# Decoder trunk on one core: carried state times C as 128-row products, decay and norm sums on VectorE, the last scaling moved

## The chip, the cores and the metric

One core of a Trainium2 chip runs the whole program. The metric is the device time of one execution in microseconds (us). The kernel before takes 1945.37 us (median of three runs, 1945.06 to 1946.57). Engines: TensorE (PE; its weight loads are PEld), VectorE (DVE), ScalarE (ACT), GpSimd (POOL), SyncE (SP, which here only issues DMAs).

## The reference

A decoder layer on a sequence of 1024 tokens with 1024 channels: layer norm, one large input projection, two token mixers side by side (a convolution branch and a Mamba-2 state space branch), a gated sum, an output projection, and a gated feed-forward block with a short convolution. The part that matters here is the state space branch, in chunks of 128 tokens, for 32 heads of 64 channels in 4 groups that share B and C:

```python
a_cs = jnp.cumsum(a, axis=-1)
decay = where(causal, exp(a_cs[..., :, None] - a_cs[..., None, :]), 0.0)
cb = einsum("bclgn,bcsgn->bcgls", cc, bc)
y_diag = einsum("bcgrls,bcsgrp->bclgrp", cb[:, :, :, None] * decay, xs)
states = einsum("bclgn,bcgrl,bclgrp->bcgrpn", bc, decay_states, xs)
...  # carry: prev = chunk_decay * prev + states
y_off = einsum("bclgn,bcgrpn,bcgrl->bclgrp", cc, prev, exp(a_cs))
return y_diag + y_off
```

`y_off` is the state carried in from the chunks before, times C, times a decay that depends on head and token. Behind it: the skip term, the gate silu(z), and an RMS norm over each group of 512 channels. In the convolution branch a layer norm over 1024 channels follows a convolution with 31 taps.

## The kernel before

The tokens are worked in two halves of 512. Activations lie transposed (channels on partitions, tokens along the free axis). Every large product is three products of float32r parts (`mm3`, L192 to L194): high times high, high times low, low times high. So a weight tile of 128x1024 is loaded by SP, its high part cast by ACT (L158) and its low part subtracted by DVE (L163; in the second half many low parts come back from DRAM). TensorE needs both.

`mixers(hh, hT)` runs the four groups of a half: projections of B, C, x with their short convolution (`conv4`), the gate z, the two halves of the convolution branch's GLU, and then `ssd_group` with four chunks. In a chunk (first half 0, second half 1; names such as m_3_1 are group and chunk):

- `px` (L646) transposes x, `pb` (L649, L650) transposes B and makes C times B.
- `ab` (L640) is a DMA that spreads the cumulated decays of 8 heads over all partitions. ACT makes the decay matrix `m` from it (L653 eight times Relu, L660 Exp), DVE multiplies it by the masked C times B (L685).
- For all but the very first chunk, ACT makes `ce` = exp(ab) (L663) and POOL multiplies it by C (L664), 128x1024.
- `py` (L690, L693): for each head, 64 output rows: the diagonal part from `xs` and `m`, then the carried part from the state `S` and `ce`, accumulated in the same PSUM bank. Two heads of a pair lie on the two halves of the output partitions.
- `pn` (L192 to L194) is the chunk's new state; DVE scales S by the chunk's decay (L702) and adds it (L705).
- DVE adds the skip term (L708, four times 128x128), multiplies by the gate (L719), ACT squares (L721), DVE sums (L722, L723).

`scaled()` of a group makes the norm: TensorE sums over partitions (L730), ACT takes the root, DVE the reciprocal (L739, `rows`), POOL issues two DMAs that send the row to DRAM and spread it over the partitions (L741, L742, `rstd`), and DVE scales x with it (L745, four times 128x512). `parts()` splits the result into high and low (ACT L759, DVE L760). In groups 1 to 3 `scaled` of the group before is called ahead of the group's chunks, and its L745 is bound behind the skip of chunk 0 by a list `held`. Group 3's own `scaled` and `parts` are called in the loop over the last gate columns, at j = 4. The next phase, `gated`, begins with the gate_b weights (`w_gb`).

The 31-tap convolution runs as 480 single operations on DVE (L577, 128x512, taps named c<-vl), which `fill` puts behind other work in small numbers (table `FILL`). `conv_norm` loads the eight convolved blocks of a half, sums them for the mean, and sums their squares (POOL: L869, L871, L881).

A scheduler sets each engine's order from the program's order, the priorities and its own estimates; the engines work their lists strictly in order. PSUM has two pools of four banks: `acc` for the projections, `sm` for everything small.

Of the kernel before, what the change touches and what calls it, by code (L numbers as in the profile page):

```python
# [8 lines left out]
F32 = mybir.dt.float32  # L9
F32R = mybir.dt.float32r  # L10
AF = mybir.ActivationFunctionType
# [52 lines left out]
def kernel(  # L64
# [557 lines left out]
    def ssd_group(pl, hh, g, xT, BT, CT, zs):  # L622
# [10 lines left out]
        for c in range(4):  # L633
# [25 lines left out]
                )  # L659
            exps.append(A.activation(out=m, in_=m, func=AF.Exp, scale=-1.0))  # L660
            if not first:
                ce = pl.tile([P, 8, P], F32, tag="ce", name=f"ce{nm}")
                A.activation(out=ce, in_=ab, func=AF.Exp)  # L663
                G.tensor_tensor(  # L664
                    out=ce, in0=ce, in1=CT[:, cs].unsqueeze(1).to_broadcast([P, 8, P]), op=ALU.mult
                )
            cbm = pl.tile([P, P], F32, tag="cbm", name=f"cbm{nm}")
            V.tensor_mul(cbm, pb[:, P : 2 * P], upper)
# [18 lines left out]
            for i in range(4):  # L687
                pair = [(2 * i + k, py[k * HP : (k + 1) * HP, i * P : (i + 1) * P]) for k in (0, 1)]
                for h, o in pair:
                    TE.matmul(o, xs[:, h * HP : (h + 1) * HP], m[:, h, :], start=True, stop=first)  # L690
                if not first:
                    for h, o in pair:
                        TE.matmul(  # L693
                            o, S[:, h * HP : (h + 1) * HP], ce[:, h, :], start=False, stop=True
                        )
            if not last:
                pn = bank(0)
                mm3(pn, lambda i: bt[:, i, :], lambda i: xsd[:, i, :], True, True)
# [7 lines left out]
            for i in range(4):  # L706
                k = PC_SD + 4 * g + i
                skip = V.scalar_tensor_tensor(  # L708
                    out=xT[:, i, cs],
                    in0=xT[:, i, cs],  # L710
                    scalar=pc[:, k : k + 1],
                    in1=py[:, i * P : (i + 1) * P],
                    op0=ALU.mult,
                    op1=ALU.add,
                )
            fill(FILL[hh][1], skip)
            while held and c == 0:
                issue_after(held.pop(), skip)
            V.tensor_mul(xT[:, :, cs], xT[:, :, cs], zs[:, :, cs])  # L719
            sq = pl.tile([P, 4, P], F32, tag="sq", name=f"sq{nm}")  # L720
# [62 lines left out]
    def mixers(hh, hT):  # L783
        pre = first_columns(hh, hT, (CT_B, CT_C, CT_X))
        with pool(f"mixers{hh}") as pl:
            time_steps(pl, hh, pre[0])
            scaled = parts = None
            for g in range(GROUPS):
                BT = conv4(pl, hh, column(hh, hT, CT_B + g) if g else pre[1], 16 + g)
                CT = conv4(pl, hh, column(hh, hT, CT_C + g) if g else pre[2], 20 + g)  # L790
                xT = pl.tile([P, 4, HALF], F32, tag="x4", bufs=2, name=f"x4_{hh}_{g}")
                for i in range(4):
                    j = 4 * g + i
                    conv4(pl, hh, column(hh, hT, CT_X + j) if j else pre[3], j, xT[:, i, :])
                zs = z_gate(pl, hh, hT, g)
                for i in (2 * g, 2 * g + 1):
                    glu(pl, hh, hT, i)
                    conv31(hh, i)
                if g:
                    scaled()  # L800
                if g == 1:
                    yT = big_tile(f"yT{hh}_0")
                if g in (1, 2):
                    parts(yT)
                split_2 = parts
                scaled, parts = ssd_group(pl, hh, g, xT, BT, CT, zs)
                if g == 3:
                    ssm_out_first(pl, hh, yT)
                    yT = big_tile(f"yT{hh}_2")
                    split_2(yT)  # L810
                    gate_first(pl, hh, hT, range(3))
            for j in range(3, 8):
                gate_first(pl, hh, hT, (j,))
                fill(FILL[hh][2], los[-1])
                if j == 4:
                    scaled()
                    parts(yT)
        return yT

    def gated(pl, hh, hT, yT, during):  # L820
# [37 lines left out]
    def conv_norm(pl, hh, place):  # L858

        squares = pl.tile([P, 2, HALF], F32, tag="sq", name=f"csq{hh}")  # L860
        stats = pl.tile([P, 2, HALF], F32, tag="stats", name=f"stats{hh}")
        mean, var = stats[:, 0, :], stats[:, 1, :]
        n = 8
        pairs = [pl.tile([P, 2, HALF], F32, tag=f"c{i}", name=f"cc{hh}_{i}") for i in range(n // 2)]
        cs = []
        for i in range(n):
            G.dma_start(pairs[i // 2][:, i % 2, :], c_scr[hh][i])
            cs.append(pairs[i // 2][:, i % 2, :])
        G.tensor_add(mean, cs[0], cs[1])  # L869
        for c in cs[2:]:  # L870
            G.tensor_add(mean, mean, c)  # L871
        pm = bank(0)
        TE.matmul(pm, mean_w, mean, start=True, stop=True)
        for i, c in enumerate(cs):
            V.tensor_tensor(out=c, in0=c, in1=pm, op=ALU.subtract)
            if i == 0:
                A.activation(out=var, in_=c, func=AF.Square)
            else:
                sq = squares[:, i % 2, :]
                A.activation(out=sq, in_=c, func=AF.Square)  # L880
                G.tensor_add(var, var, sq)  # L881
        return lambda: conv_silu(pl, cs, var, place)

    def conv_silu(pl, cs, var, place):
# [677 lines left out]
```

## Time and profile before

| | |
|---|---|
| median of three runs | 1945.37 us (1945.06 to 1946.57) |
| profiled execution | 1946.6 us, its span 1944.9 us |
| granted TensorE clock, mean | 0.997 |
| PE busy | 1920.8 us, 99% |
| DVE busy | 1640.9 us, 84% |
| ACT busy | 1104.3 us, 57% |
| POOL busy | 221.7 us, 11% |
| DMA | 398.44 MB, 205 GB/s over the span |

The span runs from the first to the last instruction of the profiled execution. A row of the view of groups reads: line, engine, operation, out<-in, shapes, count | busy us, mean ns of one | idle time of the engine just before them and what ended it. A row of the timeline reads: start, duration, engine, line, operation, and in brackets the idle time before it. The chunks of the first half lie between about 97 and 430 us, those of the second between 630 and 985, `gated` of the second half begins near 1024.

### The profile page before, as it was taken

The numbers are of one execution on the slowest core, as the hardware profiler recorded it, in microseconds if no ns is written. First come the engines' busy times: TensorE is split into PE (matmuls) and PEld (weight loads), VectorE is DVE, ScalarE is ACT, GpSimd is POOL, SyncE is SP. The second block draws the span as 40 slices with busy tenths as digits, with TensorE's granted clock in tenths as the row PEclk, the third lists the DMA queues.
The fourth block names the chain that finished last, engine by engine and source line by source line (L and its number), as shares of the span: only waits on it lengthen the run. The fifth ranks groups of instructions, "written<-read, shape, count | busy, mean of one in ns | idle before, by whom it ended". The sixth has DMA issues, their size and how long they took to land.

```text
span 1944.9 us, 26118 instructions
## 1 busy us (share of the span) xinstructions
PE 1920.8 (99%) x9452; PEld 1576.9 (81%) x9452; DVE 1640.9 (84%) x2278; ACT 1104.3 (57%) x1648; POOL 221.7 (11%) x275
## 2 busy tenths in 40 slices
PE   9999999999999999999999999999999999999998
PEld 8887888788878888878777888888888888888886
DVE  7488999897998698989978787787788888889778
ACT  6586777654525777776532535365555555553534
POOL 1001011011000111110112250011000000022010
PEclk9999999999999999999999999999999999999999
DMA  6655565547486565554464474776445555479673
GB/s 231 217 187 205 204 208 177 177 167 282 180 280 212 198 220 205 192 208 171 162 224 162 149 241 176 247 260 238 156 163 200 174 176 187 162 266 368 205 243 114
DMA packets 138194, 398.44 MB, mean 205 GB/s; under 512 B 16432, under 2 KB 16976, under 8 KB 138064
## 3 DMA queue, kind: packets, MB, share of 16 engines
q1 hardware_dynamic: 116928, 335.39, 50.0%
q0 software_dynamic: 14656, 49.83, 7.1%
q10 hardware_dynamic: 6480, 11.55, 1.6%
q8 instruction: 74, 1.21, 0.3%
q14 instruction: 56, 0.46, 0.1%
HBM read 300.61 MB, written 96.09 MB: 204 GB/s over the span
## 4 chain that ended last, share of the span: by engine, by line
PE 44%; issue 3%; DMA 2%; DVE 2%; ACT 0%; POOL 0%; DVEq 0%; ACTq 0%; POOLq 0%; SPq 0%
PE acc L194 8%; PE acc L192 8%; PE acc L193 8%; PE sm L192 7%; PE sm L193 7%; PE sm L194 7%; DMA st_wo<-wo 1%; DMA rstd<-nrm_scr 1%; DMA first_scr<-first 0%; DVE x L745 0%; DVE c L577 0%; DMA rb<-wup 0%; POOL ce L664 0%; DMA nrm_scr<-rows 0%; DVE yT_l L760 0%
## 5 line engine op out<-in xcount | busy, mean ns | idle before, releaser
L192 PE MATMUL acc<-hT_h,w_c 128*128 128x512 f32 x1000 | 391.4, 391 | 0.8 <-ACT w_c L158 0.8
L194 PE MATMUL acc<-hT_h,w_c 128*128 128x512 f32 x1000 | 389.9, 391 | 0.4 <-DMA w_c<-low_scr 0.4
L193 PE MATMUL acc<-hT_l,w_c 128*128 128x512 f32 x1000 | 390.0, 390 | 0.0
L577 DVE SCALAR_TENSOR_TENSOR c<-vl,pc,c 128x512 f32<-128x512 f32 x480 | 376.4, 805 | 6.8 <-ACT c L566 2.7
L192 PEld LDWEIGHTS acc<-hT_h,w_c 128*128 128x128 f32 x1000 | 187.8, 188 | 41.7 <-issue 1.4
L194 PEld LDWEIGHTS acc<-hT_h,w_c 128*128 128x128 f32 x1000 | 187.8, 188 | 39.8 <-DMA w_c<-low_scr 0.9
L193 PEld LDWEIGHTS acc<-hT_l,w_c 128*128 128x128 f32 x1000 | 187.8, 188 | 38.8 <-issue 0.3
L158 ACT CAST w_c<-st_c 128x1024 fp32r<-128x1024 f32 x128 | 133.8, 1046 | 131.0 <-PE acc L194 88.3
L664 POOL TENSOR_TENSOR ce<-ce,xbc 128x1024 f32<-128x1024 f32 x28 | 72.7, 2597 | 495.0 <-ACT ce L663 495.0
L1287 ACT CAST w_dn<-dr 128x1024 fp32r<-128x1024 f32 (+1 forms) x72 | 67.3, 943 | 75.7 <-DVE dr L1220 39.8
L192 PE MATMUL sm<-h1s,w_s 128*128 128x512 f32 x264 | 102.8, 389 | 0.5 <-ACT fuv L1130 0.5
L163 DVE TENSOR_TENSOR w_c<-st_c,w_c 128x1024 fp32r<-128x1024 f32 x62 | 76.9, 1240 | 30.6 <-ACT w_c L158 30.5
L193 PE MATMUL sm<-h1s,w_s 128*128 128x512 f32 x264 | 102.7, 389 | 0.0
L194 PE MATMUL sm<-h1s,w_s 128*128 128x512 f32 x264 | 102.2, 389 | 0.0
L653 ACT ACTIVATE m<-ab,acs 128x128 f32<-128x128 f32 x256 | 78.3, 391 | 26.5 <-PE sm L690 24.8
L1288 DVE TENSOR_TENSOR w_dn<-dr,w_dn 128x1024 fp32r<-128x1024 f32 (+1 forms) x72 | 77.7, 1087 | 4.7 <-ACT w_dn L1287 4.6
L527 DVE SCALAR_TENSOR_TENSOR x<-u,pc,x 128x512 f32<-128x512 f32 x96 | 74.8, 793 | 3.6 <-ACT x L525 3.5
L194 PE MATMUL acc<-h1b_h,w_ue 128*128 128x512 f32 x176 | 68.7, 395 | 0.5 <-DVE w_ue L163 0.5
L192 PE MATMUL acc<-h1b_h,w_ue 128*128 128x512 f32 x176 | 68.7, 391 | 0.0
L193 PE MATMUL acc<-h1b_l,w_ue 128*128 128x512 f32 x176 | 68.6, 390 | 0.0
L192 PE MATMUL sm<-h1b_h,w_s 128*128 128x512 f32 x176 | 68.5, 389 | 0.0
L193 PE MATMUL sm<-h1b_l,w_s 128*128 128x512 f32 x176 | 68.5, 389 | 0.0
(376 smaller groups left out, 4636.8 us busy)
## 6 DMA issues: line engine op xcount, KB each, us to landing
st_c<-wcol SPq DMA_DIRECT2D x128, 512.0 KB, 4.4
low_scr<-w_c SPq DMA_DIRECT2D x64, 512.0 KB, 2.9
w_c<-low_scr SPq DMA_DIRECT2D x64, 512.0 KB, 4.5
ab<-acs_scr SPq DMA_DIRECT2D x32, 512.0 KB, 4.1
dr<-wdown SPq DMA_DIRECT2D x55, 256.0 KB, 5.0
st_wo<-wo SPq DMA_DIRECT2D x24, 512.0 KB, 4.3
st_ue<-wup SPq DMA_DIRECT2D x22, 512.0 KB, 3.6
first_scr<-first ACTq DMA_DIRECT2D x44, 256.0 KB, 3.0
```

The costliest lines, as they stand in the source:

```text
L158: casts.append(A.copy(w[:, 0, :], st))
L163: sub.tensor_tensor(out=w[:, 1, :], in0=st, in1=w[:, 0, :].bitcast(F32), op=ALU.subtract)
L192: TE.matmul(ps, wa(0), xa(0), start=start, stop=False, skip_group_check=more)
L193: TE.matmul(ps, wa(0), xa(1), start=False, stop=False, skip_group_check=more)
L194: TE.matmul(ps, wa(1), xa(0), start=False, stop=stop, skip_group_check=more)
L527: V.scalar_tensor_tensor(out=o, in0=u[:, k : k + HALF], scalar=pc[:, wc + k : wc + k + 1], in1=o, op0=ALU.mult, op1=ALU.add,)
L577: step = V.scalar_tensor_tensor(out=c, in0=v[:, k : k + HALF], scalar=pc[:, wc + k : wc + k + 1], in1=c, op0=ALU.mult, op1=ALU.add,)
L653: A.activation(out=m[:, h, :], in_=ab[:, h, :], func=AF.Relu, scale=-1.0, bias=acs[:, c, 8 * g + h : 8 * g + h + 1],)
L664: G.tensor_tensor(out=ce, in0=ce, in1=CT[:, cs].unsqueeze(1).to_broadcast([P, 8, P]), op=ALU.mult)
L1287: A.copy(w[:, 0, cs], src)
L1288: V.tensor_tensor(out=w[:, 1, cs], in0=src, in1=w[:, 0, cs].bitcast(F32), op=ALU.subtract)
```

## The change

In a chunk with a carried state, TensorE now makes S times C first, without decay, as four products with 128 rows of output into a bank of its own, `pq` (L671 of the new file). `ce` is half as large (128 channels x 4 x 128): two DMAs on SP load the cumulated decay of the head that each channel belongs to (L665), ACT takes Exp (L668), DVE multiplies the bank by it (L675). The skip operation adds `ce` instead of the bank `py` (L714), and one more DVE operation adds `py` (L723). `ce` still has one buffer. POOL's multiplication is gone. In `conv_norm` the sums go from POOL to DVE (L881, L883, L893). The scaling of group 2 is bound behind the skip of chunk 2 of group 3, not chunk 0; `scaled` and `parts` of group 3 are called before the loop over j = 3 to 7.

```diff
-                ce = pl.tile([P, 8, P], F32, tag="ce", name=f"ce{nm}")
-                A.activation(out=ce, in_=ab, func=AF.Exp)
-                G.tensor_tensor(
-                    out=ce, in0=ce, in1=CT[:, cs].unsqueeze(1).to_broadcast([P, 8, P]), op=ALU.mult
+                ce = pl.tile([P, 4, P], F32, tag="ce", name=f"ce{nm}")
+                by_two = acs_scr[hh][r : r + 8, :].rearrange("(i k) l -> k i l", k=2)
+                for k in range(2):
+                    SY.dma_start(
+                        ce[k * HP : (k + 1) * HP], by_two[k].partition_broadcast(HP)
+                    )
+                A.activation(out=ce, in_=ce, func=AF.Exp)
+                pq = bank(0)
+                for i in range(4):
+                    TE.matmul(
+                        pq[:, i * P : (i + 1) * P], S[:, i * P : (i + 1) * P], CT[:, cs],
+                        start=True, stop=True,
+                    )
+                V.tensor_tensor(
+                    out=ce, in0=pq.rearrange("p (i l) -> p i l", i=4), in1=ce, op=ALU.mult
                 )
...
-                    TE.matmul(o, xs[:, h * HP : (h + 1) * HP], m[:, h, :], start=True, stop=first)
-                if not first:
-                    for h, o in pair:
-                        TE.matmul(
-                            o, S[:, h * HP : (h + 1) * HP], ce[:, h, :], start=False, stop=True
-                        )
+                    TE.matmul(o, xs[:, h * HP : (h + 1) * HP], m[:, h, :], start=True, stop=True)
...
-                    in1=py[:, i * P : (i + 1) * P],
+                    in1=py[:, i * P : (i + 1) * P] if first else ce[:, i],
...
+            if not first:
+                skip = V.tensor_tensor(
+                    out=xT[:, :, cs],
+                    in0=xT[:, :, cs],
+                    in1=py.rearrange("p (i l) -> p i l", i=4),
+                    op=ALU.add,
+                )
             fill(FILL[hh][1], skip)
-            while held and c == 0:
+            while held and c == (2 if g == 3 else 0):
...
                     gate_first(pl, hh, hT, range(3))
+                    scaled()
+                    parts(yT)
             for j in range(3, 8):
                 gate_first(pl, hh, hT, (j,))
                 fill(FILL[hh][2], los[-1])
-                if j == 4:
-                    scaled()
-                    parts(yT)
...
-        G.tensor_add(mean, cs[0], cs[1])
+        V.tensor_add(mean, cs[0], cs[1])
         for c in cs[2:]:
-            G.tensor_add(mean, mean, c)
+            V.tensor_add(mean, mean, c)
...
-                G.tensor_add(var, var, sq)
+                V.tensor_add(var, var, sq)
```

The order on the engines moves at three places on which the prediction rests. The first is VectorE in the last group of the second half. Before, from the skip of chunk 0 to the masking of chunk 1 (m_3_1), with the scaling of the group before (L745) between:

```order
L708 SCALAR_TENSOR_TENSOR x_1_3_7817<-x_1_3_7817,pc,sm_8300 128x128 x4
L745 SCALAR_TENSOR_TENSOR x_1_2_6990<-x_1_2_6990,pc,rstd_2_8248 128x512 x4
L577 SCALAR_TENSOR_TENSOR c_5_7731<-vl_5_7730,pc,c_5_7731 128x512
L705 TENSOR_TENSOR state_106<-state_106,sm_8317 128x512
L670 TENSOR_TENSOR xs_3_1_8369<-sm_8346,dtv 128x512
L676 TENSOR_TENSOR whole_3_1_8372<-sm_8346,wds 128x512
L668 TENSOR_TENSOR cbm_3_1_8367<-sm_8351,upper 128x128
L719 TENSOR_TENSOR x_1_3_7817<-x_1_3_7817,zs_3_7970 128x4x128
L577 SCALAR_TENSOR_TENSOR c_5_7731<-vl_5_7730,pc,c_5_7731 128x512
L685 TENSOR_TENSOR m_3_1_8354<-m_3_1_8354,cbm_3_1_8367 128x1024
```

In the changed kernel the same scaling (now L758) on VectorE stands behind chunk 2, ahead of the masking of chunk 3:

```order
L714 SCALAR_TENSOR_TENSOR x_1_3_7817<-x_1_3_7817,pc,ce_3_2_8440 128x128 x4
L577 SCALAR_TENSOR_TENSOR c_5_7731<-vl_5_7730,pc,c_5_7731 128x512
L711 TENSOR_TENSOR state_106<-state_106,sm_8472 128x512
L681 TENSOR_TENSOR xs_3_3_8528<-sm_8499,dtv 128x512
L723 TENSOR_TENSOR x_1_3_7817<-x_1_3_7817,sm_8463 128x4x128
L758 SCALAR_TENSOR_TENSOR x_1_2_6990<-x_1_2_6990,pc,rstd_2_8248 128x512 x4
L577 SCALAR_TENSOR_TENSOR c_6_8334<-vl_6_8333,pc,c_6_8334 128x512
L679 TENSOR_TENSOR cbm_3_3_8526<-sm_8504,upper 128x128
L577 SCALAR_TENSOR_TENSOR c_5_7731<-vl_5_7730,pc,c_5_7731 128x512
L732 TENSOR_TENSOR x_1_3_7817<-x_1_3_7817,zs_3_7970 128x4x128
L577 SCALAR_TENSOR_TENSOR c_6_8334<-vl_6_8333,pc,c_6_8334 128x512
L696 TENSOR_TENSOR m_3_3_8506<-m_3_3_8506,cbm_3_3_8526 128x1024
```

The scaling that waits for `rstd` has moved by two chunks, and each chunk has L675 and L723 more on VectorE.

The second place is VectorE at the end of the second half's mixers, from the reciprocal of the last norm to its scaling (w_gb are the weights of the next phase, c the taps). Before:

```order
L577 SCALAR_TENSOR_TENSOR c_6_8334<-vl_6_8333,pc,c_6_8334 128x512 x20
L739 RECIPROCAL rows_3_9006<-rows_3_9006 128x128
L163 TENSOR_TENSOR w_gb_0_9146<-st_gb_0_9144,w_gb_0_9146 128x1024
L745 SCALAR_TENSOR_TENSOR x_1_3_7817<-x_1_3_7817,pc,rstd_3_9005 128x512 x4
L760 TENSOR_TENSOR yT_2_l<-x_1_3_7817,yT_2_h 128x1024
L163 TENSOR_TENSOR w_gb_1_9178<-st_gb_1_9176,w_gb_1_9178 128x1024
```

The same place of VectorE in the changed kernel:

```order
L752 RECIPROCAL rows_3_8928<-rows_3_8928 128x128
L577 SCALAR_TENSOR_TENSOR c_6_8334<-vl_6_8333,pc,c_6_8334 128x512
L577 SCALAR_TENSOR_TENSOR c_7_8984<-vl_7_8983,pc,c_7_8984 128x512
L577 SCALAR_TENSOR_TENSOR c_6_8334<-vl_6_8333,pc,c_6_8334 128x512
L577 SCALAR_TENSOR_TENSOR c_7_8984<-vl_7_8983,pc,c_7_8984 128x512
L577 SCALAR_TENSOR_TENSOR c_6_8334<-vl_6_8333,pc,c_6_8334 128x512 x13
L163 TENSOR_TENSOR w_gb_0_9146<-st_gb_0_9144,w_gb_0_9146 128x1024
L758 SCALAR_TENSOR_TENSOR x_1_3_7817<-x_1_3_7817,pc,rstd_3_8927 128x512 x4
L773 TENSOR_TENSOR yT_2_l<-x_1_3_7817,yT_2_h 128x1024 x2
L163 TENSOR_TENSOR w_gb_1_9178<-st_gb_1_9176,w_gb_1_9178 128x1024
```

Seventeen taps now stand between the reciprocal and the scaling that waits for its trip through DRAM.

The third place is ScalarE in the last group of the second half, between the copies of two projections (ya) and the Exp of chunk 1's m. Before:

```order
L772 COPY ya_1_8621<-acc_8596 128x512
L653 ACTIVATE m_3_1_8354<-ab_3_1_8344,acs 128x128 x8
L663 ACT_TABLE_LOAD
L663 ACTIVATE ce_3_1_8364<-ab_3_1_8344 128x1024
L660 ACTIVATE m_3_1_8354<-m_3_1_8354 128x1024
```

ScalarE in the changed kernel:

```order
L785 COPY ya_1_8621<-acc_8596 128x512
L668 ACT_TABLE_LOAD
L668 ACTIVATE ce_3_1_8364<-ce_3_1_8364 128x512
L653 ACTIVATE m_3_1_8354<-ab_3_1_8344,acs 128x128 x8
L660 ACTIVATE m_3_1_8354<-m_3_1_8354 128x1024
```

The Exp of the newly loaded decay now stands ahead of the eight Relus that m needs.

## Prediction

> **What bounds the kernel now.** I read the page first, then the busy time by stretches of 20 us, then the timelines of TensorE and VectorE where a stretch falls short.
>
> ```profile
> span 1944.9 us, 26118 instructions
> PE 1920.8 (99%) x9452; PEld 1576.9 (81%) x9452; DVE 1640.9 (84%) x2278; ACT 1104.3 (57%) x1648; POOL 221.7 (11%) x275
> ```
> TensorE is busy for 99% of the span. A change can pay in two ways only: fewer or cheaper products, or the few places where TensorE stands still. Of the stretches from 20 to 1060 us these are all that hold less than 20.00 us of PE, and the last is full but at a lower clock:
>
> ```profile
> 140.00:160.00 20.00, 18.84 (x110) 15.33 (x109) 20.00 (x32) 16.33 (x27) 2.98 (x1) 1.00 0.43 155
> 340.00:360.00 20.00, 19.21 (x108) 15.57 (x107) 18.94 (x28) 15.83 (x26) 2.67 (x1) 1.00 0.62 220
> 840.00:860.00 20.00, 18.84 (x109) 15.10 (x108) 19.36 (x33) 18.12 (x35) 2.98 (x2) 1.00 0.57 206
> 940.00:960.00 20.00, 18.16 (x107) 14.84 (x106) 19.96 (x30) 7.28 (x16) 3.12 (x2) 1.00 0.30 112
> 960.00:980.00 20.00, 17.58 (x115) 14.30 (x116) 19.89 (x32) 13.51 (x24) 2.88 (x1) 1.00 0.60 198
> 1020.00:1040.00 20.00, 15.59 (x67) 12.31 (x67) 17.81 (x13) 7.96 (x10) 13.04 (x9) 0.97 0.49 183
> 1040.00:1060.00 20.00, 20.00 (x77) 16.27 (x77) 19.43 (x25) 4.44 (x6) 0.00 (x0) 0.86 0.38 132
> ```
> Columns: PE, PEld, DVE, ACT, POOL busy, then granted clock, DMA share, GB/s. Where PE falls short, DVE is nearly full: VectorE is what TensorE waits for there. The shortfalls are 1.16 + 0.79 + 1.16 (three single chunks), 1.84 + 2.42 (the last group of the second half), and 4.41 just past 1020. The last is the largest:
>
> ```profile
> 1030.41 0.50 PE L194 MATMUL acc<-hT_h,w_gb 128*128 128x512 f32 x1 [0.91 <-DVE w_gb L163]
> ...
> 1035.76 0.39 PE L193 MATMUL acc<-hT_l,w_gb 128*128 128x512 f32 x1
> 1039.65 0.80 PE L194 MATMUL acc<-hT_h,w_gb 128*128 128x512 f32 x1 [3.50 <-DVE w_gb L163]
> ...
> 1045.73 0.39 PE L193 MATMUL acc<-hT_l,w_gb 128*128 128x512 f32 x1
> ```
> From 1035.76 to 1045.73 stand 15 products. At the usual 0.227 us from start to start they take 3.4 us; they took 9.97. So 6.6 us are lost: 3.5 of waiting and some 3 at half clock behind it. With 0.9 us at 1030 that makes 7.5. The cause is on DVE:
>
> ```profile
> 1010.01 0.95 DVE L739 RECIPROCAL rows<-rows 128x128 f32<-128x128 f32 x1
> ...
> 1022.12 3.78 DVE L745 SCALAR_TENSOR_TENSOR x<-x,pc,rstd 128x512 f32<-128x512 f32 x4 [7.03 <-DMA rstd<-nrm_scr]
> ...
> 1028.05 2.31 DVE L163 TENSOR_TENSOR w_gb<-st_gb,w_gb 128x1024 fp32r<-128x1024 f32 x1
> ...
> 1038.37 1.22 DVE L163 TENSOR_TENSOR w_gb<-st_gb,w_gb 128x1024 fp32r<-128x1024 f32 x1
> ```
> Between the reciprocal and the scaling lies a trip through DRAM of 11.2 us, and DVE sits idle for 7.03 of them. Then, while POOL adds up the norm's sums, L163 takes 2.31 us instead of 1.22.
>
> The Trainium skill, "TensorE: Matmul & The Clock Gate", Part 1, says that the array drops to half clock after an idle window of about 3.4 us and needs a busy one to come back. This trace agrees: 3.50 us of idle here were followed by products at half pace, the shorter waits below were not.
>
> The other waits end with the masked decay matrix m, also DVE's:
>
> ```profile
> 947.75 0.44 PE L690 MATMUL sm<-m,xs 128*64 128x128 f32 x4 [1.83 <-DVE m L685]
> ...
> 962.86 0.44 PE L690 MATMUL sm<-m,xs 128*64 128x128 f32 x4 [1.28 <-DVE m L685]
> ...
> 979.13 0.44 PE L690 MATMUL sm<-m,xs 128*64 128x128 f32 x4 [1.14 <-DVE m L685]
> ```
>
> **Part by part. The products of the state** (28 chunks have them).
>
> ```profile
> 119.06 0.39 PE L693 MATMUL sm<-ce,state 128*64 128x128 f32 x4
> 119.28 0.39 PE L690 MATMUL sm<-m,xs 128*64 128x128 f32 x4
> ```
> ```profile
> 41.20 0.97 PE L398 MATMUL sm<-quads,dtc 128*128 128x32 f32 x8
> 42.01 0.48 PE L194 MATMUL acc<-hT_h,w_c 128*128 128x512 f32 x1
> ```
> Two 64-wide products of a pair of heads run side by side: the four records of L693 take 0.22 us to the next group, four pairs 0.88 us a chunk. The new four products with 128 weight columns have no row of their own; nearest is L398, four such float32 products with fewer moving columns, 0.81 us and 0.1 more on re-entering the stream. So 0.91 against 0.88: halving the instructions gains nothing. **+0.03 x 28 = +0.8 us.** Bounds: 0 (the extra entry hides) and +6 (if 128 moving columns cost twice the step over L398's, 0.2 us a chunk).
>
> **The decay moves from POOL to DVE.** The multiplication of 128x1024 on POOL goes. DVE gets two operations of 128x512 a chunk: state product times decay, and the sum with the bank of the diagonal part.
>
> ```profile
> 937.66 4.89 DVE L745 SCALAR_TENSOR_TENSOR x<-x,pc,rstd 128x512 f32<-128x512 f32 x4 [2.24 <-DMA rstd<-nrm_scr]
> 942.48 0.74 DVE L577 SCALAR_TENSOR_TENSOR c<-vl,pc,c 128x512 f32<-128x512 f32 x1
> 943.14 0.68 DVE L705 TENSOR_TENSOR state<-state,sm 128x512 f32<-128x512 f32 x1
> 943.74 0.68 DVE L670 TENSOR_TENSOR xs<-sm,dtv 128x512 f32<-128x512 f32 x1
> ```
> ```profile
> 465.74 2.74 DVE L745 SCALAR_TENSOR_TENSOR x<-x,pc,rstd 128x512 f32<-128x512 f32 x4 [3.05 <-DMA rstd<-nrm_scr]
> ```
> ```profile
> 937.82 2.87 POOL L664 TENSOR_TENSOR ce<-ce,xbc 128x1024 f32<-128x1024 f32 x1 [4.56 <-ACT ce L663]
> ```
> ```profile
> L664 POOL TENSOR_TENSOR ce<-ce,xbc 128x1024 f32<-128x1024 f32 x28 | 72.7, 2597 | 495.0 <-ACT ce L663 495.0
> ```
> A 128x512 product out of a bank costs 0.60 us to the next start (943.14 to 943.74): 2 x 0.60 x 28 = +33.6 us of DVE. But POOL's multiplication is not free to DVE now: the same four scalings took 4.89 us beside it and 2.74 without it, 2.15 us more. A POOL operation hurts between nothing (DVE idle) and 2.15 us; I take 1.5, nearer the upper end since DVE is full in these stretches: -42 us. DVE's load in the chunks so stays within some 10 us in total of what it was.
>
> The Trainium skill, "SBUF — State Buffer", section "SBUF: two separate sides", says that GpSimd and a VectorE operation with two SBUF inputs lock a shared port pair for a whole instruction. By that rule all of the 72.7 us of L664 could be given back to DVE; the rows above show 2.15 of 2.87, and TensorE gains from it only where it waits.
>
> **The scalings move.** Order of DVE: in the last group of the second half L745 with its 2.24 us of waiting stood before chunk 1's m, and now stands between chunks 2 and 3. From m of chunk 0 to m of chunk 1 DVE then has, from the rows above, 8 taps at 0.66, seven operations at 0.60, two weight splits and m at 1.14, and 1.5 of small ones: 14.4 us. TensorE has there, by its order, 30 and 22 products of 0.227, and the chunk's own groups (0.9 each for diagonal and carried products, an estimated 1.6 for state products and transposes): 15.2 us. Before it was short by 1.83. For chunks 2 and 3 the same count gives 12.2 against 12.0 and 15.1 against 17.1. So the 4.25 us of these three waits shrink, to about 1: **-3.2 us** (bounds 0 and -4.2).
>
> At the end of the half, 17 taps now stand between the reciprocal and the scaling: 17 x 0.66 + 1.14 = 12.4 us over the trip's 11.2. The idle 7.03 is covered, and without POOL's adds the weight splits are short again: **-7 us of the 7.5** (bounds -3, if only the half clock goes, and -7.5). If the trip takes over 12.4, DVE waits the rest and TensorE still has some 5 us in hand.
>
> **Norm sums.**
>
> ```profile
> L881 POOL TENSOR_TENSOR stats<-stats,csq 128x512 f32<-128x512 f32 x14 | 23.2, 1660 | 56.5 <-ACT csq L880 55.5
> L871 POOL TENSOR_TENSOR stats<-stats,cc 128x512 f32<-128x512 f32 x12 | 21.3, 1771 | 1.0 <-DMA cc<-c_scr 0.3
> ```
> 28 additions at 0.60 are +16.8 us of DVE, spread over 130 us in which TensorE shows no wait but the one counted; they are hidden by its products, and POOL's slowing of DVE (1.09 us a weight split) goes. **0.** If that cover were gone, one addition is 0.6 us.
>
> **The other three waits** (3.1 us) lie in chunks whose order changes little: **-1.0** (0 to -3.1).
>
> **A new load.** The decay rows are loaded again, as two DMAs a chunk on SP, into one buffer that is free only after the previous chunk's L714 on DVE. Weight loads queue behind them on SP; ScalarE's Exp waits for them, and in one place of the order stands ahead of the next m's Relu.
>
> ```profile
> L663 ACT ACTIVATE ce<-ab 128x1024 f32<-128x1024 f32 x28 | 29.6, 1058 | 7.3 <-DMA ab<-acs_scr 7.2
> L653 ACT ACTIVATE m<-ab,acs 128x128 f32<-128x128 f32 x256 | 78.3, 391 | 26.5 <-PE sm L690 24.8 <-DMA ab<-acs_scr 1.7
> ```
> ```profile
> ab<-acs_scr SPq DMA_DIRECT2D x32, 512.0 KB, 4.1
> ...
> rows<-h_scr POOLq DMA_DIRECT2D x8, 512.0 KB, 8.4
> ```
> After m of chunk 0, L714 ends at 2.5 us; Exp (half of 1.06), eight Relus (2.4) and the Exp of m (1.06) follow the landing, and m is due at 13.3. So a landing of up to 6.8 us is hidden. The nearest row, the same data for the same engine, is 4.1. L675 on DVE waits for this Exp and for TensorE's product; behind it stand the state's scaling and weight splits, for which TensorE waits. A chunk also takes five turns of the four small PSUM banks, not four, so that the next transposes can wait for L675. For a few such delays I take **+2.0**; bounds 0 and +22 (below).
>
> ```profile
> L660 ACT ACT_TABLE_LOAD x17 | 21.8, 1283 | 0.3
> ```
> ACT's Exp is halved, 0.5 x 28 = -15 us, and six table loads more stand in its order, 6 x 1.28 = +8: nothing, since ACT is busy for 57%.
>
> **Sum**: 0.8 - 3.2 - 7.0 - 1.0 + 2.0 = -8.4 us. Against the profiled execution, 1946.6 (span 1944.9 and 1.7 around it), that is 1938.2; the median of the runs is 1945.37, 1.2 lower, so **1937.0**.
>
> **Rivals.**
> *The wait only moves* (0.18). VectorE carries 33.6 + 16.8 = 50 us more instructions. If POOL cost it only 0.3 us an operation, each chunk grows by 1.2 - 0.3 = 0.9 us, and in the 8 or so chunks of the stretches above, where DVE has no slack, 7 us come back as waits: 0.8 - 7.0 + 7 = +1, 1946. For it: DVE is busy for 19.9 of 20 there. Against: the 2.15 us measured.
> *Slower: the decay load comes late* (0.15). The load is in pieces of 512 bytes, not 4 KB, on a queue with the weights. It decides from 6.8 us to landing. At 8.4, the slowest row above, each chunk is 1.6 us late, less 0.8 of TensorE's slack: 0.8 x 28 = 22. With -7.0 and +0.8: +16, 1961. Against: 4.1 for twice the bytes.
> *All waits go* (0.07). 15 us of waits and half clock and +0.8: 1931, and below if nothing new waits.
> A single late load that leaves TensorE idle for 3.5 us would cost another 3 of half clock, as at 1039.65.
>
> **How the numbers follow.** The forecast (0.60) covers 1931 to 1941. 0.2%, 3.9 us, is about what a measurement of this kernel can tell. Faster: 0.60 + 0.07 = 0.67; same 0.18; slower 0.15. The range takes in the forecast and the moved wait, 1930 to 1948, and leaves out the late load and a little below.
>
> **What would show it.** Right: PE full from 1020 to 1060 at clock 1.00; no 7 us wait before L758; L671's four products about 0.9 us; taps near 0.75 us everywhere. Wrong: L675 or the Exp of ce waiting for its DMA with PE idle behind it; PE stretches short at new places; L671 well over 1 us a chunk.

## The result, and the profile after

The changed kernel takes 1937.65 us (median of six runs, 1935.11 to 1942.36) against 1945.97 for the kernel before (six runs, 1943.72 to 1948.22): a ratio of 0.9959 with a 95% interval of 0.9943 to 0.9975, about 8 us. The profiled execution took 1936.25, its span is 1934.2. In the tables of experiments below, three executions that took 2752 to 9790 us are left out of the medians.

The head of the changed kernel's page: span, and busy time of each engine.

```profile
span 1934.2 us, 25804 instructions
PE 1919.7 (99%) x9228; PEld 1577.6 (82%) x9228; DVE 1624.7 (84%) x2362; ACT 1101.6 (57%) x1654; POOL 101.6 (5%) x219
```

VectorE has 84 instructions more and is busy for 16 us less: the operations that it had before got shorter. The 480 taps show it best. Their group, in the kernel before and then in the changed kernel:

```profile
L577 DVE SCALAR_TENSOR_TENSOR c<-vl,pc,c 128x512 f32<-128x512 f32 x480 | 376.4, 805 | 6.8 <-ACT c L566 2.7
```

```profile
L577 DVE SCALAR_TENSOR_TENSOR c<-vl,pc,c 128x512 f32<-128x512 f32 x480 | 345.9, 744 | 4.5 <-ACT c L566 1.2
```

The stretches of the changed kernel that answer to those of the prediction, and one new (columns as there: PE, PEld, DVE, ACT, POOL, then granted clock, DMA share, GB/s):

```profile
140.00:160.00 20.00, 20.00 (x104) 16.40 (x103) 20.00 (x37) 19.86 (x36) 0.00 (x0) 1.00 0.61 214
340.00:360.00 20.00, 20.00 (x100) 16.25 (x100) 14.08 (x25) 16.45 (x26) 0.00 (x0) 1.00 0.56 203
660.00:680.00 20.00, 16.05 (x84) 12.92 (x83) 13.37 (x26) 17.64 (x30) 0.00 (x0) 0.91 0.42 146
840.00:860.00 20.00, 20.00 (x118) 16.23 (x118) 18.55 (x30) 16.70 (x30) 0.00 (x0) 1.00 0.65 215
940.00:960.00 20.00, 20.00 (x112) 16.62 (x111) 19.16 (x35) 16.12 (x34) 0.00 (x0) 1.00 0.63 227
960.00:980.00 20.00, 20.00 (x118) 16.20 (x117) 20.00 (x38) 11.06 (x19) 0.00 (x0) 1.00 0.63 204
1020.00:1040.00 20.00, 20.00 (x90) 16.57 (x89) 18.84 (x27) 6.18 (x8) 0.00 (x0) 1.00 0.45 156
1040.00:1060.00 20.00, 20.00 (x90) 16.53 (x90) 13.42 (x16) 4.64 (x6) 0.00 (x0) 1.00 0.32 118
```

Every stretch that was short before is full now, at clock 1.00. One that was full before (20.00 from 660 to 680) lacks 3.95 us of work and runs at a granted clock of 0.91: with 0.09 x 20 = 1.8 us for the clock it loses 5.75. That is the second half's first group, chunk 1. SP's queue, ScalarE and TensorE of the changed kernel at that place:

```profile
652.72 0.59 SPq L665 DMA_DIRECT2D ce<-acs_scr  x1
...
654.48 0.58 SPq L665 DMA_DIRECT2D ce<-acs_scr  x1
```

```profile
654.29 2.45 ACT L653 ACTIVATE m<-ab,acs 128x128 f32<-128x128 f32 x8 [1.28 <-PE sm L701]
660.16 1.28 ACT L668 ACT_TABLE_LOAD   x1 [3.42 <-issue]
661.45 0.63 ACT L668 ACTIVATE ce<-ce 128x512 f32<-128x512 f32 x1
...
665.43 1.06 ACT L660 ACTIVATE m<-m 128x1024 f32<-128x1024 f32 x1
```

```profile
667.80 1.09 PE L701 MATMUL sm<-m,xs 128*64 128x128 f32 x16 [3.01 <-DVE m L696]
669.84 0.79 PE L192 MATMUL sm<-xsd,bt 128*128 128x512 f32 x1 [0.94 <-ACT bt L692]
670.43 0.63 PE L193 MATMUL acc<-hT_l,w_c 128*128 128x512 f32 x1
```

Read from below: TensorE waits 3.01 us for m and 0.94 for bt and then runs at half pace. m's Exp (665.43) stands behind the Exp of ce on ScalarE; between the two lie another activation (L537) and two table loads of 1.28 us each. The Exp of ce waits until 660.16 for the decay rows. Their two DMAs left at 652.72, when the one buffer came free, and, behind two weight loads, at 654.48; the second landed 5.6 us later, at 660.08. (The row names no releaser, only "issue"; the time of landing is what ties the wait to the load.) It is the late load of the prediction's slower rival, in one chunk of the 28.

VectorE of the changed kernel at the end of the half:

```profile
997.59 0.95 DVE L752 RECIPROCAL rows<-rows 128x128 f32<-128x128 f32 x1 [1.59 <-ACT rows L751]
998.45 12.75 DVE L577 SCALAR_TENSOR_TENSOR c<-vl,pc,c 128x512 f32<-128x512 f32 x17
1012.32 1.23 DVE L163 TENSOR_TENSOR w_gb<-st_gb,w_gb 128x1024 fp32r<-128x1024 f32 x1 [1.11 <-ACT w_gb L158]
1013.46 2.73 DVE L758 SCALAR_TENSOR_TENSOR x<-x,pc,rstd 128x512 f32<-128x512 f32 x4
...
1019.59 3.10 DVE L577 SCALAR_TENSOR_TENSOR c<-vl,pc,c 128x512 f32<-128x512 f32 x4
```

The 17 taps take 12.75 us and the scaling (L758) finds its row there: no wait in brackets, where 7.03 us stood before.

### The profile page after: what moved, and what is told of

Same layout as the page of the kernel before. It is cut to its first block, busy times and chain, and to the rows that moved or that the text cites. A ratio compares the mean times of both kernels' runs of the same rounds, so it can differ in the third digit from the quotient of the medians.

```text
span 1934.2 us, 25804 instructions
## 1 busy us (share of the span) xinstructions
PE 1919.7 (99%) x9228; PEld 1577.6 (82%) x9228; DVE 1624.7 (84%) x2362; ACT 1101.6 (57%) x1654; POOL 101.6 (5%) x219
## 4 chain that ended last, share of the span: by engine, by line
PE 96%; DMA 1%; DVE 1%; ACT 1%; issue 0%; SPq 0%; POOL 0%; DVEq 0%; ACTq 0%; POOLq 0%
PE acc L194 23%; PE acc L192 23%; PE acc L193 23%; PE sm L192 7%; PE sm L193 7%; PE sm L194 7%; PE sm L701 2%; PE sm L671 1%; PE acc L508 1%; PE sm L646 1%; DMA st_wo<-wo 1%; PE acc L474 0%; PE sm L276 0%; DMA first_scr<-first 0%; PE sm L650 0%
## 5 line engine op out<-in xcount | busy, mean ns | idle before, releaser
L577 DVE SCALAR_TENSOR_TENSOR c<-vl,pc,c 128x512 f32<-128x512 f32 x480 | 345.9, 744 | 4.5 <-ACT c L566 1.2
L158 ACT CAST w_c<-st_c 128x1024 fp32r<-128x1024 f32 x128 | 133.9, 1047 | 160.0 <-PE acc L194 105.1
L527 DVE SCALAR_TENSOR_TENSOR x<-u,pc,x 128x512 f32<-128x512 f32 x96 | 70.0, 740 | 5.0 <-ACT x L525 5.0
L192 PE MATMUL sm<-h1b_h,w_s 128*128 128x512 f32 x176 | 68.5, 389 | 0.0
L194 PE MATMUL sm<-h1b_h,w_s 128*128 128x512 f32 x176 | 68.5, 389 | 0.0
```

The lines of the kernel that those rows point to most:

```text
L158: casts.append(A.copy(w[:, 0, :], st))
L192: TE.matmul(ps, wa(0), xa(0), start=start, stop=False, skip_group_check=more)
L194: TE.matmul(ps, wa(1), xa(0), start=False, stop=stop, skip_group_check=more)
L527: V.scalar_tensor_tensor(out=o, in0=u[:, k : k + HALF], scalar=pc[:, wc + k : wc + k + 1], in1=o, op0=ALU.mult, op1=ALU.add,)
L577: step = V.scalar_tensor_tensor(out=c, in0=v[:, k : k + HALF], scalar=pc[:, wc + k : wc + k + 1], in1=c, op0=ALU.mult, op1=ALU.add,)
```

## The experiments

Each kernel ran five times or more beside the kernel before; that one's median was 1946.33, 1946.19 and 1947.0 in the three sets. The last column is (1 - ratio) x 1946. Each profile below is of one of these executions, and not always of a typical one: that of state_only took 1942.69 us and that of ce_on_dve 1945.70, in each case the slowest of those in the median.

| kernel | edits it has | median us | ratio to before (95%) | us less |
|---|---|---|---|---|
| changed | all, ce loaded | 1937.65 | 0.9959 (0.9943 to 0.9975) | 8.0 |
| state_only | state | 1937.21 | 0.9951 (0.9937 to 0.9964) | 9.5 |
| move_only | scalings moved | 1940.22 | 0.9965 (0.9953 to 0.9978) | 6.8 |
| norm_only | norm sums | 1939.53 | 0.9964 (0.9951 to 0.9976) | 7.0 |
| ce_on_dve | multiplication of ce on VectorE | 1940.54 | 0.9972 (0.9961 to 0.9982) | 5.4 |
| ce2 | all, two buffers of ce | 1939.79 | 0.9965 (0.9952 to 0.9977) | 6.8 |
| from_ab | all, no load | 1933.78 | 0.9937 (0.9925 to 0.9950) | 12.3 |
| exp_later | all, Exp of ce behind m's | 1933.79 | 0.9934 (0.9922 to 0.9946) | 12.8 |
| ab_dum | from_ab and a GpSimd multiplication | 1952.98 | 1.0035 (1.0021 to 1.0049) | -6.8 |
| ab_held0 | from_ab, group 2's scaling back | 1935.08 | 0.9943 (0.9931 to 0.9956) | 11.1 |
| ab_late | from_ab, group 3's scaling back | 1934.91 | 0.9944 (0.9932 to 0.9957) | 10.9 |
| ab_pool_norm | from_ab, norm sums back | 1933.13 | 0.9933 (0.9920 to 0.9945) | 13.0 |
| ab_unmoved_pool | from_ab, all three back | 1938.48 | 0.9956 (0.9943 to 0.9969) | 8.6 |

### One part at a time

The part on the state alone is the changed kernel with these lines as they were before:

```diff
-            while held and c == (2 if g == 3 else 0):
+            while held and c == 0:
...
-                    scaled()
-                    parts(yT)
             for j in range(3, 8):
...
+                if j == 4:
+                    scaled()
+                    parts(yT)
...
-        V.tensor_add(mean, cs[0], cs[1])
+        G.tensor_add(mean, cs[0], cs[1])
...
```

The other two additions of the norm sums go back to GpSimd in the same way.

> Only the part on the carried state: products of 128 rows, decay on VectorE, the new load; norm sums stay on GpSimd, the scalings stay where they were. Theory: the three single waits go (-3 us), the two late waits of group 3 shrink by 1 to 2 with GpSimd out of the way, the products cost +1 to +2, the late load +5, and the end of the half stays as before (wait of 3 to 4 us for w_gb and half clock behind it): +1 to +3 us, 1946 to 1949. Rival (GpSimd's slowing of VectorE was what TensorE waited for): VectorE gets back some 43 us of lengthened operations, all waits for m go, -6 us or more, 1940 or less.

Measured: 9.5 us less; the theory fell and its rival held. Two stretches of it in group 3 and one at the end of the half, then VectorE in group 3 and at the end:

```profile
940.00:960.00 20.00, 20.00 (x111) 16.64 (x111) 20.00 (x35) 13.63 (x28) 0.00 (x0) 1.00 0.61 187
960.00:980.00 20.00, 20.00 (x117) 16.20 (x117) 20.00 (x38) 10.95 (x19) 0.00 (x0) 1.00 0.68 212
1020.00:1040.00 20.00, 17.18 (x69) 13.70 (x69) 19.72 (x16) 6.50 (x9) 12.51 (x7) 0.91 0.44 150
```

```profile
937.02 2.73 DVE L758 SCALAR_TENSOR_TENSOR x<-x,pc,rstd 128x512 f32<-128x512 f32 x4
...
1024.99 6.88 DVE L577 SCALAR_TENSOR_TENSOR c<-vl,pc,c 128x512 f32<-128x512 f32 x4
```

The scaling of group 2 still stands at chunk 0 here. It takes 2.73 us where it took 4.89, its wait of 2.24 is gone, and group 3 is full: all three waits for m went without the move. At the end, four taps beside GpSimd's norm sums take 6.88 us; in the changed kernel four take 3.10 (above). There 2.82 us and some clock are still lost in this execution, less than before; it is 5.5 us above the median, so what the other four lost there is not known. The median is no worse than the changed kernel's: beside this part the other two edits brought nothing that these runs can tell, and the wait at 660, 3.95 us there, is 1.59 in this profile.

> Only the two scalings moved; the carried state and the norm sums as before. Theory: the end of the half is cured, -5 to -7 us (TensorE full from 1020 to 1060 at clock 1.00, no VectorE wait of 7 us for rstd), and the three waits of group 3 shrink, -2 to -3 us: -7 to -10 us, 1936 to 1939. Rival (the norm sums on GpSimd made w_gb late): the weight splits stay at 2.3 us beside them, waits of 1 to 2 us for w_gb stay, -3 to -5 us, 1941 to 1943.

Its edit is the reverse of the first two pieces of the diff above, in the kernel before. Measured: 6.8 us less.

```profile
940.00:960.00 20.00, 19.69 (x113) 15.90 (x112) 19.89 (x28) 11.63 (x23) 3.81 (x2) 1.00 0.30 106
960.00:980.00 20.00, 18.17 (x114) 15.09 (x115) 19.89 (x32) 10.06 (x18) 2.88 (x1) 1.00 0.70 224
1020.00:1040.00 20.00, 20.00 (x90) 16.57 (x89) 19.61 (x18) 5.94 (x8) 10.36 (x6) 1.00 0.45 155
```

The end of the half is cured, though GpSimd still adds there for 10.36 us; group 3 goes from 4.26 us lost to 2.14. Both stretches moved as the theory had it; the time, 1940.22, lies between its range (1936 to 1939) and the rival's (1941 to 1943).

> The kernel before with one edit: the norm sums on VectorE. The scaling of group 3 stays late. Theory (two causes in a row at the end of the half, either cured is enough): the weight splits are 1.2 us again, the wait of 0.9 goes and that of 3.5 shrinks below 2 with no half clock behind it, 4 to 7.5 us less than before, 1939 to 1942. Rival (the trip of rstd alone makes TensorE wait): 0 to 1.5 us less, 1944.5 to 1946.

```diff
-        G.tensor_add(mean, cs[0], cs[1])
+        V.tensor_add(mean, cs[0], cs[1])
...
-            G.tensor_add(mean, mean, c)
+            V.tensor_add(mean, mean, c)
...
-                G.tensor_add(var, var, sq)
+                V.tensor_add(var, var, sq)
```

Measured: 7.0 us less. Its stretch, and its scaling on VectorE:

```profile
1020.00:1040.00 20.00, 20.00 (x90) 16.57 (x89) 18.40 (x24) 8.63 (x11) 0.54 (x1) 1.00 0.70 258
```

```profile
1021.38 2.74 DVE L745 SCALAR_TENSOR_TENSOR x<-x,pc,rstd 128x512 f32<-128x512 f32 x4 [6.93 <-DMA rstd<-nrm_scr]
```

VectorE still idles for 6.93 us, and TensorE loses nothing in this stretch. So the end of the half needed two things in a row, the trip of rstd and GpSimd's adds behind it; either cure is enough.

### GpSimd or the form of the products

> The kernel before with one edit: the multiplication of ce by C (128x1024) runs on VectorE, not on GpSimd. The products keep their old form, no load is added, nothing else moves by hand. VectorE gets 28 x 1.14 = 32 us more, nearly what the change gives it (33.6). Theory (GpSimd's multiplication lengthened VectorE's operations): the waits for m in group 3 and the single ones go, the end of the half stays, 4 to 8 us less than before, 1938 to 1942. Rival (the form of the products, C first in a bank of its own, gave the gain): no gain, 1945 to 1948.

```diff
-                G.tensor_tensor(
+                V.tensor_tensor(
                     out=ce, in0=ce, in1=CT[:, cs].unsqueeze(1).to_broadcast([P, 8, P]), op=ALU.mult
```

Measured: 5.4 us less. One letter changed, and group 3 is full but for 0.02 us:

```profile
340.00:360.00 20.00, 18.60 (x105) 14.94 (x104) 15.08 (x25) 16.43 (x27) 0.00 (x0) 1.00 0.58 202
...
940.00:960.00 20.00, 19.98 (x114) 16.15 (x114) 19.93 (x34) 12.06 (x23) 0.00 (x0) 1.00 0.58 186
960.00:980.00 20.00, 20.00 (x116) 16.50 (x115) 19.89 (x34) 12.84 (x24) 0.00 (x0) 1.00 0.62 211
```

The multiplication itself is now this row of VectorE:

```profile
L664 DVE TENSOR_TENSOR ce<-ce,xbc 128x1024 f32<-128x1024 f32 x28 | 34.2, 1223 | 10.2 <-ACT ce L663 10.2
```

VectorE is busy for 1628.6 us here and for 1640.9 before: 12.3 us less with 34.2 us of work more. Its other operations so got about 46 us shorter, some 1.6 us for each multiplication that left GpSimd. That ce itself is ready sooner is no rival cause: in the kernel before no wait of TensorE ends with ce.

Among the chunks, single waits of 1.40, 1.40 and 1.66 us stand at 254, 346 and 839 us. Two end with ScalarE's cast of a weight tile (L158), one with m; with the new form of the products (8.6 to 9.5 us less) they are not there. By the medians most of that part's gain is GpSimd's and 3 to 4 us are left for the form; but the intervals overlap, and the form also halves the Exp on ScalarE, so that this share is not shown.

The reverse test: from_ab (below), with work for GpSimd that nobody reads. The order of instructions on the other engines is the same to the row, and none of them waits for the added work or for what it reads.

```diff
+                dum = pl.tile([P, 8, P], F32, tag="dum", name=f"dum{nm}")
+                G.tensor_tensor(
+                    out=dum, in0=ab, in1=CT[:, cs].unsqueeze(1).to_broadcast([P, 8, P]), op=ALU.mult
+                )
```

> The version that makes ce from ab (1933.8 us), with one multiplication of 128x1024 a chunk added on GpSimd whose result nobody reads; the order on the other engines is the same. Theory (contention): GpSimd's multiplication lengthens VectorE's operations by some 40 us in all, as before the change, and the waits for m come back in the chunks where VectorE is full: +3 to +8 us, 1937 to 1942. Rival (the products in a bank of their own, or the smaller Exp, took the waits away): no wait comes back, 1933 to 1935.

Measured: 1952.98 against 1933.78, 19 us more, over twice what the theory asked and slower than the kernel before. Busy time of from_ab, then of ab_dum:

```profile
PE 1918.9 (99%) x9228; PEld 1576.1 (82%) x9228; DVE 1625.5 (84%) x2362; ACT 1105.2 (57%) x1670; POOL 101.7 (5%) x219
```

```profile
PE 1925.1 (99%) x9228; PEld 1578.8 (81%) x9228; DVE 1669.8 (86%) x2362; ACT 1106.3 (57%) x1670; POOL 185.8 (10%) x247
```

The same 2362 instructions of VectorE take 44.3 us more beside 84.1 us of GpSimd: 1.58 us for each of the 28. The Trainium skill, "SBUF — State Buffer", section "SBUF: two separate sides", says that GpSimd and a VectorE operation with two inputs in SBUF cannot both hold the shared port pair, and that the later one is blocked for the whole instruction; by that rule, as an estimate, up to 84 us could be lost, and the run shows about half. It falls on the operations with two such inputs: from from_ab to ab_dum the 96 operations of a convolution at L527 go from a mean of 742 to 923 ns and the taps from 744 to 796, while the multiplication out of the bank, which has one input in PSUM, stays (674 and 675 ns).

The two longest groups of TensorE's waits in ab_dum (total us, times, longest):

```profile
PE sm L193 <- DVE xsd L694: 5.7, 5, 2.6
PE sm L702 <- DVE m L697: 2.4, 1, 2.4
```

So waits for VectorE come back, but most are for other results of it than m: the theory named the engine rightly and the tile wrongly. Of the 17.0 us between the two spans some 11 are such idle time and 3.6 the half clock in two stretches (0.91 from 660 and from 960); the rest is not accounted for. That adding GpSimd's work costs 19 us where taking it away brought 5.4 has a plain reading: ab_dum leaves VectorE 44.3 us more to do, while ce_on_dve, which pays for the multiplication on VectorE, leaves it 12.3 less. No run tests this.

### The late load

> The changed kernel with two buffers for ce, so that the decay rows of a chunk are loaded a chunk earlier. Theory (late load): in the changed kernel's profile ScalarE waits for the decay rows in chunk 2 of group 0 of the second half, the mask m comes late behind it, and TensorE loses 3.0 + 0.9 us and then some 1.6 us at half clock (664 to 673 us). With the second buffer this goes: 5 to 6 us less than the changed kernel, about 13.5 us less than before (1932), and no wait of TensorE over 1 us between 640 and 680. Rival (a single event): that landing was late in the profiled execution alone; the median stays 8 to 9 us under before (1937). Rival (m itself): the order on ScalarE, not the load, makes m late; the 3 us wait stays.

```diff
-                ce = pl.tile([P, 4, P], F32, tag="ce", name=f"ce{nm}")
+                ce = pl.tile([P, 4, P], F32, tag="ce", bufs=2, name=f"ce{nm}")
```

Measured: 6.8 us less than before, no better than the changed kernel. The stretch and the wait stay:

```profile
660.00:680.00 20.00, 15.72 (x82) 12.65 (x82) 13.06 (x25) 16.95 (x28) 0.00 (x0) 0.91 0.50 169
```

```profile
ACT L668 <- DMA ce<-acs_scr: 3.8, 1, 3.8
```

The edit did not do what it was meant to: the scheduler used the second buffer to put the Exp a chunk earlier too, so that the next chunk's ce, still waited for, stood at the same place ahead of m. The wait follows the order on ScalarE; more buffers with the order held fixed were not tried.

> The changed kernel without the new load: ce is made from ab, which already holds the decays of all eight heads on all partitions, by two Exp of 64 partitions each. Theory (late load): nothing to wait for, so again 5 to 6 us less than the changed kernel, about 13.5 us less than before (1932); the 28 extra Exp of about 0.6 us each hide on ScalarE, which is busy for 57%. Rival (ScalarE gets late): the extra 0.6 us a chunk stands ahead of m and shows as waits of TensorE for m in the full stretches; 8 us less than before or worse (1937 and up). Rival (a single event): 8 to 9 us less than before.

```diff
-                by_two = acs_scr[hh][r : r + 8, :].rearrange("(i k) l -> k i l", k=2)
                 for k in range(2):
-                    SY.dma_start(
-                        ce[k * HP : (k + 1) * HP], by_two[k].partition_broadcast(HP)
-                    )
-                A.activation(out=ce, in_=ce, func=AF.Exp)
+                    ks = slice(k * HP, (k + 1) * HP)
+                    A.activation(out=ce[ks], in_=ab[ks, k::2, :], func=AF.Exp)
```

> The changed kernel with the Exp of ce ordered behind the Exp of the same chunk's m on ScalarE; the load stays as it is. Theory (the load is late, and m stood behind it): 3 to 5 us less than the changed kernel, 1933 to 1935, no wait of 3 us around 665. Rival (the late load then holds up VectorE's multiplication of the bank and all behind it): no gain, 1937 or more.

```diff
-                A.activation(out=ce, in_=ce, func=AF.Exp)
+                issue_after(A.activation(out=ce, in_=ce, func=AF.Exp), exps[-1])
```

Measured: 1933.78 and 1933.79, both 3.9 us below the changed kernel's median; every run of exp_later (up to 1934.92) lies below every run of the changed kernel (from 1935.11). The stretch of from_ab, that of exp_later, and m's Exp in exp_later, 5.4 us earlier than in the changed kernel, with the load untouched:

```profile
660.00:680.00 20.00, 19.80 (x110) 16.29 (x109) 20.00 (x37) 19.77 (x39) 0.00 (x0) 1.00 0.56 188
```

```profile
660.00:680.00 20.00, 20.00 (x111) 16.59 (x110) 18.25 (x32) 17.95 (x35) 0.00 (x0) 1.00 0.62 204
```

```profile
660.03 1.06 ACT L660 ACTIVATE m<-m 128x1024 f32<-128x1024 f32 x1
```

So the load is fast enough for the multiplication that uses it; it was late only for the Exp that m stood behind. Of the 5.4 us the wait for the load is 3.42; the rest is the Exp of ce itself (0.63) and its table load (1.28), which no longer stand ahead of m.

### Undoing one part, without the load's noise

Three kernels take from_ab and put one part back, a fourth all three.

> The same version with the scaling of group 2 bound behind the skip of chunk 0 of group 3 again, not chunk 2. Theory (the part on the state alone cured group 3): within 1.5 us of 1933.8, and no wait of TensorE over 0.5 us from 930 to 985. Rival (the prediction's step: the moved scaling took 3.2 us away): two or three waits for m of 1 to 2 us come back, 1936 to 1937.

Measured: 1935.08; no wait comes back.

```profile
940.00:960.00 20.00, 20.00 (x111) 16.62 (x110) 20.00 (x36) 12.49 (x24) 0.00 (x0) 1.00 0.55 177
960.00:980.00 20.00, 20.00 (x118) 16.24 (x117) 19.82 (x37) 10.55 (x19) 0.00 (x0) 1.00 0.64 193
```

> The same version with the scaling and the split of group 3 in the loop at j = 4 again; norm sums stay on VectorE. Theory (order): VectorE waits 5 to 7 us for rstd, and TensorE loses 3 to 7 us for w_gb around 1030, half clock included: 1937 to 1941. Rival (the norm sums on GpSimd made w_gb late): with them on VectorE nothing is lost, 1933 to 1935.

Measured: 1934.91. VectorE waits again, shorter than expected, and TensorE loses nothing by it; the rival held.

```profile
1014.40 2.74 DVE L755 SCALAR_TENSOR_TENSOR x<-x,pc,rstd 128x512 f32<-128x512 f32 x4 [3.56 <-DMA rstd<-nrm_scr]
```

> The same version with the norm sums on GpSimd again. Theory: VectorE's operations are lengthened by some 20 us over 130 us, but the early scaling leaves TensorE enough work: 0 to +1.5 us, 1933.8 to 1935.3. Rival (the norm sums matter by themselves): waits for w_gb of 1 to 3 us come back, 1936 to 1938.

Measured: 1933.13, and the end of the half is full, though the scaling beside GpSimd takes 6.87 us for 2.73:

```profile
1009.74 6.87 DVE L755 SCALAR_TENSOR_TENSOR x<-x,pc,rstd 128x512 f32<-128x512 f32 x4
```

```profile
1020.00:1040.00 20.00, 20.00 (x90) 16.56 (x89) 19.47 (x24) 5.21 (x8) 0.01 (x1) 1.00 0.51 158
```

> The version with ce from ab, the norm sums on GpSimd and both scalings where they were before: the part on the state alone, without its load. Theory (the end of the half needs one of the two other parts, either will do): TensorE loses some 4 us for w_gb around 1030, half clock included, 1937 to 1939. Rival (with VectorE's load in the chunks lighter, the end cures itself): 1933 to 1935.

Measured: 1938.48, 4.7 above from_ab, as the theory's time. Its stretch shows only 1.48 us of it:

```profile
1020.00:1040.00 20.00, 18.52 (x81) 14.71 (x80) 19.64 (x18) 7.12 (x10) 9.46 (x5) 1.00 0.46 151
```

The half clock that the theory counted does not show. In this profile, an execution at the median, TensorE waits another 2.4 us near 1880, for weights (w_dn) of a phase that no edit touches, and some 1 us more than from_ab in single waits at 100 and 660. So the theory's time came out, but only 1.48 us of it by the theory's mechanism; the rest is luck.

ab_pool_norm has the lowest median, but from_ab, exp_later and it cannot be told apart by their intervals. All three beat the changed kernel's median by about 4 us.

## Why the prediction was right, point by point

The time (1937.0 forecast, 1937.65 measured) and the direction held. That they agree so closely is partly luck, since among the terms two errors cancelled: the waits removed were worth 3.7 us more than forecast, and the late load cost 3.75 more.

| term | forecast us | profile of the changed kernel | what the runs say of it |
|---|---|---|---|
| end of the half | -7.0 | -7.5, all of it | two sufficient cures |
| three waits of group 3 | -3.2 | -4.3, all | the state part's, not the move's |
| three other waits | -1.0 | -3.1, all | the state part's; not told apart further |
| load, late ce | +2.0 | +5.75 | 3.9 in the medians |
| products | +0.8 | +0.02 in one chunk, 0.6 for 28 | not told apart in the medians |
| norm sums | 0 | no wait there | -7.0 alone, about 0 beside the move |

**Products.** L671's four calls take 0.81 us to the next start, not 0.91:

```profile
661.67 1.05 PE L671 MATMUL sm<-xbc,state 128*128 128x128 f32 x8
662.48 0.48 PE L193 MATMUL acc<-hT_l,w_c 128*128 128x512 f32 x1
```

Halving the instructions gained nothing visible, as forecast: in the chunk near 948 us the diagonal and carried products took 1.90 us before (947.75 to 949.65), and now take 1.03 (948.57 to 949.60), L671's 0.81 and 0.08 on re-entering the stream, 1.92 in all. The span fell by 10.7 us; the four rows above it make -9.2 in idle time and clock. The other 1.5 are not traced.

**The decay and VectorE.** The price taken for a GpSimd multiplication, 1.5 us, is what ab_dum (1.58) and ce_on_dve (some 1.6) show. That decides against the rival in which the wait only moves, which needed 0.3. What failed is the step from there: "DVE's load in the chunks so stays within some 10 us" was read as no change for TensorE, and the gain was then given to the moved scalings. state_only, ab_held0 and above all ce_on_dve, which has no other edit, show that group 3's three waits go when GpSimd's multiplication goes, wherever the scaling stands; move_only takes away half of them, ab_held0 shows that this half is not needed. The prediction's own row, 4.89 us beside GpSimd and 2.74 without, was the sign of it: 2.15 us at the very place where TensorE waits 1.83.

**The other three waits** were sized too small by 2.1. "Chunks whose order changes little" is true, but the durations in them changed. They were also misread: the prediction says that the other waits end with m, and only the one at 140 does. The one at 340 (0.79 us) ends with ScalarE's cast of a weight tile, and the 1.16 us at 840 are 0.57 for xsd, 0.44 for a weight load from DRAM and 0.15 for m. The state part removes nearly all of them (0.17 us stays at 840 in state_only); in ce_on_dve, without the new form, TensorE still waits at both places. The one at 140 is gone even in norm_only, which makes no edit there, so its cause is open.

**The end of the half.** The size was right, and the mechanism as told for this kernel (17 taps over the trip). But the step that put the norm sums at 0 failed as a statement about that edit: norm_only alone brings 7.0. The two share one loss, which the sum rightly counted once; either edit removes it, so it belongs to neither alone.

**The late load** had its mechanism and its point of decision right (6.8 us; here the rows were there 7.4 us after the buffer came free, 652.72 to 660.16), and the half clock behind it. Of the 7.4 us 1.76 were the second DMA's place behind two weight loads in SP's queue, and 5.6 its landing. It struck one chunk in the profile, not 28, and cost 3.9 us in the medians against 2.0. It is the one term that the change could have done without.

**The rivals.** "All waits go" (1931) is nearly what from_ab and exp_later are, at 1934.

## What to carry to other kernels

An operation on GpSimd had a price on VectorE here: 1.58 us of VectorE for 3.0 us of GpSimd. Where VectorE is full and TensorE waits for it, taking the operation over on VectorE can pay even though VectorE gets nearly as much work (here 1.22 us an operation); compare the same line's mean duration with and without GpSimd beside it before arguing about order. When several edits aim at one loss, price each alone and together: three parts here bring 6.8, 7.0 and 8.6 us alone and 12.3 together. And a load that is early enough for its user can be late for what stands behind it in the fixed order of an engine: here a changed order brought 3.9 us and a second buffer nothing.

## What the runs showed of the hardware

The half clock needs less idle time than the prediction's rows let one think. ce_on_dve, TensorE at the end of the half:

```profile
1036.43 0.50 PE L194 MATMUL acc<-hT_h,w_gb 128*128 128x512 f32 x1 [2.00 <-DVE w_gb L163]
...
1038.08 0.63 PE L194 MATMUL acc<-hT_h,w_gb 128*128 128x512 f32 x1
...
1041.07 0.44 PE L192 MATMUL acc<-hT_h,w_gb 128*128 128x512 f32 x1
```

After 2.00 us of idle time and 1.6 of full pace come 3.0 us at half pace (1038.08 to 1041.07, seven products). The Trainium skill, "TensorE: Matmul & The Clock Gate", Part 1, puts the idle window at about 3.4 us; here 2.00 was enough, and in ab_dum 2.19 at 958.8 was, but 2.37 at 118.3 was not. In ce_on_dve, in ab_dum and in state_only (2.81 us of idle time at 1031.3) the half pace began 3.6 to 4.1 us after the idle time began. The length of the idle time alone so does not decide; what else does is open.

Single waits come and go: near 1880 us, which no edit touches, TensorE waits 1.6 to 1.7 us in six of the profiles, and not at all in those of the kernel before and the changed one. Runs of one kernel spread over 1.5 to 7 us. A single profile so shows mechanisms; only the medians of several runs price them.
